# A two-layer diffusion trunk on one core: row sums for four scale tiles in the opening, and a fixed order of splits and norm operations at four later places

## The chip, the cores and the metric

The kernel runs on one core of one Trainium2 chip. The metric is the device time of one execution in microseconds (us), lower is better. The core has a matrix engine (TensorE, PE; its weight loads are listed apart as PEld), a vector engine (VectorE, DVE), a scalar engine (ScalarE, ACT), GpSimd (POOL) and the queue of SyncE (SP), which issues most of the DMAs. Matrix products write PSUM, whose eight banks hold 128 x 512 words each.

## The reference

256 context tokens and 256 latent tokens of width 1024 pass through two layers. Layer 0 mixes tokens with a two-directional mLSTM, layer 1 with multi-head latent attention (MLA); each mixer is followed by a gated convolutional FFN, and around each sub-layer stands an adaptive LayerNorm, whose shift, scale and gate come from a condition vector:

```python
def _modulation(cond, w, b):
    m = jax.nn.silu(cond) @ w + b
    return jnp.split(m[:, None, :], 6, axis=-1)      # shift, scale, gate, shift, scale, gate

for i in range(DEPTH):                               # DEPTH = 2
    ml = _modulation(c, ada_w[i], ada_b[i])          # latent
    mc = _modulation(c_ctx[None, :], ada_w[i], ada_b[i])   # context
    hl = x * (1 + ml[1]) + ml[0]
    hc = xc * (1 + mc[1]) + mc[0]
    yl, yc = mlstm(hl, hc) if i == 0 else mla(hl, hc)
    x = layer_norm(ALPHA * x + ml[2] * yl)
    f = conv_ffn(x * (1 + ml[4]) + ml[3])
    x = layer_norm(ALPHA * x + ml[5] * f)
    ...                                              # xc the same in layer 0
```

The mLSTM starts with `h @ w_up` (1024 to 2048 columns) and ends with `... @ w_out`; the MLA ends with its own `w_out`. In the kernel these products are called up, mout and aout, the FFN's fin0, fout0, fin1 and fout1.

## The kernel before

Everything is float32. Each operand x of a product is split in two parts, hi, rounded to the format of the matrix engine, and lo = x - hi, and a product is three matrix products (`mm3`: hi hi, hi lo, lo hi). For weights, hi is a cast on ACT (L340) and lo a subtraction on DVE (L343). `Stream` handles this for all weights in one fixed order: `_load` issues the DMA of the next 128 x 1024 tile into a free raw buffer, `_split` makes the two parts, `use` hands out a tile and splits up to `AHEAD` = 8 tiles in advance, and `pump(limit)` splits up to an index. Three buffers "w" hold split tiles; tiles marked wide go to "wu" in a larger pool.

The order of instructions on PE, DVE, ACT and SP is written out by hand in the opening (`manual_schedule`), on PE also from fout0 to the first part of `mla`. Elsewhere a planner orders each engine by the order of the program and its own estimate of times; `high_priority`, `issue_after` and `keep_in_program_order` bind it.

**The opening** (`start_up`) forms h of the first norm tile by tile and multiplies with six columns of w_up's blocks. For each of the eight 128-row tiles f:

- `load(f)`: two 512 KB tiles of the modulation weights (`adaw`, four k-blocks each of 128 shift and 128 scale columns), the transposed tokens `xT`, and the weights `raw0`.
- `ada_hi`, `ada_lo` or `ada_split`: both modulation tiles are split (ACT cast, DVE subtraction).
- `ada_rows` (L501): 16 products, the condition (4 columns: hi and lo of the two conditions) as stationary operand, 256 moving columns each; `ada_copy` (ACT) and `ada_T` (two transposes on PE) make columns of them, `ada_cols` adds the bias (DVE).
- `mod`: `mod_tile` applies shift and scale, half on DVE and half on ACT, then the split of h.
- `wsplit`: the split of the six weight blocks, ACT and DVE.
- `part(f, ms)`: three products of 512 columns for each block m, 18 for a tile, in six PSUM banks `ps`.

`warm(n)` issues n products of zeros. The other modulation columns are computed later in the background: `ada_bg` (L538) multiplies a transposed weight tile with the condition, broadcast to all rows (`bc`), and sums along the row on DVE; `tick` takes such steps from `bg2` at a rate n2 per product group (`ADA_U`, `ADA_Q`, `ADA_M`, `ADA_F`).

**mout** multiplies the normed heads with 16 weight tiles, for context (`pc`) and then latent tokens (`pl`); in its first half the last head (`head(3)`, `post`) is still being computed. `after0` is the norm behind it: `ln_rows`, then `ln_T`, which transposes (`zT`, L1255), scales (`zm`, L1262, L1264) and splits (`h`, L1267, L1268) the eight column blocks, two at a time; `tail` selects the variant in which the second block of a pair is scaled on DVE. `ctx_T` in `mla` is the same for the context tokens of layer 1.

**mla** forms keys, values and queries (`queries`, `qn`, L1756), then runs eight heads: `scores`, `trans` (transposes PT and their split), `attend` (o). It yields the list `oT` when head 6 is done and again after head 7; the caller issues aout in between, with `TAIL["aout"]` = 7 of the eight k-blocks held back for the end. Behind it, `st.limit = fi + QA` and `st.pump(fi + QC)` govern how many tiles of fin1 are split before and after the norm of aout.

Of the kernel before, what the change touches and what calls it, by code (L numbers as in the profile page):

```python
# [7 lines left out]
F32 = mybir.dt.float32  # L8
# [28 lines left out]
QA, QB, QC = 2, 4, 6  # L37
# [8 lines left out]
NUP = 6  # L46

# [86 lines left out]
def _pack(i):  # L134
# [73 lines left out]
    for k, v in parts.items():  # L208
# [21 lines left out]
                                     ).reshape(8, 2, 128, 1024),  # L230
# [8 lines left out]
class Stream:  # L239
# [73 lines left out]
    def _split(self):  # L313
# [19 lines left out]
        if key[0] == "gates":  # L333
# [42 lines left out]
class K:  # L376
# [98 lines left out]
    def ada_hi(self, f, h):  # L475
        hi, lo = [self.pool.tile([128, 1024], F32R, tag="u", name="adas", bufs=NU) for _ in range(2)]
        self.nc.scalar.copy(hi, self.adaw[f, h])
        self.adas[f, h] = hi, lo

    def ada_lo(self, f, h):  # L480
        hi, lo = self.adas[f, h]
        self.nc.vector.tensor_sub(lo, self.adaw.pop((f, h)), hi)
# [3 lines left out]

    def ada_split(self, f, h):
        hi, lo = [self.pool.tile([128, 1024], F32R, tag="u", name="adas", bufs=NU) for _ in range(2)]
        w = self.adaw.pop((f, h))
        for c in self.cuts(f):  # L490
            self.split(hi[:, c], lo[:, c], w[:, c])
        self.adas[f, h] = hi, lo

    def ada_rows(self, f):

        nc = self.nc
        self.adap[f] = pr = self.ps("adar")
        for k in range(8):
            c = slice((k % 4) * 256, (k % 4 + 1) * 256)
            for x in self.adas[f, k // 4]:  # L500
                nc.tensor.matmul(pr[0:4, 0:256], self.condr[:, k, :], x[:, c],  # L501
                                 start=k == 0 and x is self.adas[f, 0][0], stop=k == 7 and x is self.adas[f, 1][1])
        del self.adas[f, 0], self.adas[f, 1]

    def ada_copy(self, f):
        self.adar[f] = r = self.s2("adarow")
        self.nc.scalar.copy(r[0:4, 0:256], self.adap[f][0:4, 0:256])

    def ada_T(self, f):
        r = self.adar.pop(f)  # L510
        for i in range(2):
# [3 lines left out]
    def ada_cols(self, f):  # L515
        nc = self.nc
        t = self.tiny(4, "adt").rearrange("p (c b) -> p c b", c=2)
        p = self.adap.pop(f)[:, 256:264].rearrange("p (c b) -> p c b", c=2)
        b = self.smc("ada_b").rearrange("p (c f) -> p c f", c=2)[:, :, f:f + 1].to_broadcast([128, 2, 2])
        nc.vector.tensor_tensor(t, p[:, :, 2:4], b, op=ALU.add)  # L520
        nc.vector.tensor_tensor(self.mod0[:, :, f, :], p[:, :, 0:2], t, op=ALU.add)
# [41 lines left out]

    def ada_all(self, items):

        nc = self.nc
        self.bc = []
        for j in range(2):
            r = self.pool.tile([128, 1024], F32, tag="acc", name="bc", bufs=2)
            self.gate(r[0:1, 0:1])  # L570
            nc.sync.dma_start(r, self.a["crow"][j:j + 1, :].to_broadcast([128, 1024]))
            self.bc.append(r)
# [6 lines left out]
        for r in self.bc:  # L579
            nc.scalar.activation(r, r, AF.Silu)  # L580
# [23 lines left out]
    def start_up(self):  # L604
# [8 lines left out]
        self.adaw, self.adas, self.adap, self.adar, self.xT = {}, {}, {}, {}, []  # L613

        def load(f):
            for h in range(2):
                t = self.uf("adaw")
                for c in self.cuts(f):
                    nc.sync.dma_start(t[:, c], self.a["adaf"][f, h][:, c])
                self.adaw[f, h] = t  # L620
            x = self.s2("xT")
            nc.sync.dma_start(x, self.a["tokT"][f])
            self.xT.append(x)
            tag, bufs = ("ar", 2) if f in (3, 4) else ("raw", NRAW)
            r = self.pool.tile([128, 1024], F32, tag=tag, name="raw0", bufs=bufs)
            nc.sync.dma_start(r[:, :NUP * 128], st.ws[st.ids["upf", f, 0][0], :, :NUP * 128])
            raws.append(r)
# [1409 lines left out]
```

## Time and profile before

| what | value |
|---|---|
| median of 3 runs | 1383.55 us (1381.83 to 1386.48) |
| profiled execution, time / span | 1382.18 / 1380.4 us |
| instructions in the span | 19253 |
| busy: PE, DVE, ACT, POOL | 98%, 77%, 51%, 9% |
| DMA | 291.86 MB, mean 211 GB/s |

Times in the trace count from the start of the span. A row of a group names line, engine, operation, output and input tile, shapes and count, then busy time and the mean of one, then the idle time before it and what ended it. A matrix product's busy time runs to its modelled end, and products overlap; their spacing is what they cost. A row of the waits reads: engine and line that waited, what ended the wait, total us, number of waits, the longest. A row of windows gives, for a stretch, its length, busy time and number of instructions of PE, PEld, DVE, ACT and POOL, then granted clock of PE (1.00 is full), busy share of the DMA engines and GB/s.

### The profile page before, as it was taken

The page shows a single profiled execution, that of the slowest core. Times are in us where ns is not written, and L with a number is a line of the kernel's source. Part 1 is how long each engine was busy: PE and PEld are TensorE (multiplying, and loading weights), DVE is VectorE, ACT ScalarE, POOL GpSimd, SP SyncE. Part 2 cuts the span into 40 slices and gives each one's busy share as a digit, 9 for nine tenths or more (in the row PEclk, how much of TensorE's full clock was granted, in tenths as well). Part 3 has the DMA queues.
Part 4 walks back from the last instruction along what each step waited for, and adds up shares of the span by engine and source line. Part 5 has one row for each costly group of instructions (what it writes and reads, how often), then busy time and mean ns, then how long its engine had stood idle before and what let it go on. Part 6 is the DMA issues. An engine that isn't in the chain of part 4 may idle for free.

```text
span 1380.4 us, 19253 instructions
## 1 busy us (share of the span) xinstructions
PE 1355.3 (98%) x6966; PEld 1146.1 (83%) x6966; DVE 1063.3 (77%) x1722; ACT 705.5 (51%) x1197; POOL 122.5 (9%) x215
## 2 busy tenths in 40 slices
PE   8999999999999999999999999999999999999997
PEld 5788888888788888878798888888879888899986
DVE  6698856687688697779789878668887888877773
ACT  6695443445544545375643433334566665555560
POOL 0032000011011011110002000001100010000000
PEclk9999999999999999999999999999999999999999
DMA  9679848788666374656737867636866415467650
GB/s 362 221 275 326 298 171 254 233 285 291 221 208 202 110 230 148 225 193 214 258 130 267 283 220 248 224 115 194 257 217 204 152 69 176 138 190 231 205 185 31
DMA packets 88334, 291.86 MB, mean 211 GB/s; under 512 B 11656, under 2 KB 12296, under 8 KB 88240
## 3 DMA queue, kind: packets, MB, share of 16 engines
q1 hardware_dynamic: 62128, 215.64, 46.6%
q0 software_dynamic: 17472, 57.57, 13.5%
q10 hardware_dynamic: 8640, 17.44, 3.4%
q8 instruction: 54, 0.88, 0.3%
q14 instruction: 40, 0.33, 0.1%
HBM read 260.02 MB, written 30.58 MB: 211 GB/s over the span
## 4 chain that ended last, share of the span: by engine, by line
PE 90%; DVE 5%; ACT 2%; DMA 2%; issue 1%; DVEq 0%; SPq 0%; ACTq 0%
PE fin L404 9%; PE fin L405 9%; PE fin L406 9%; PE y L1444 7%; PE tok L404 6%; PE tok L406 6%; PE tok L405 6%; PE qk L404 4%; PE qk L406 4%; PE qk L405 4%; PE y L405 3%; PE y L406 3%; PE y L404 3%; PE up L404 2%; PE up L405 2%; PE up L406 2%
## 5 line engine op out<-in xcount | busy, mean ns | idle before, releaser
L343 DVE TENSOR_TENSOR w<-raw,w 128x1024 fp32r<-128x1024 f32 (+1 forms) x285 | 342.9, 1206 | 149.2 <-ACT w L340 146.4
L340 ACT CAST w<-raw 128x1024 fp32r<-128x1024 f32 (+1 forms) x285 | 295.7, 1039 | 295.6 <-PE fin L406 87.1
L405 PE MATMUL fin<-h,w 128*128 128x256 f32 (+1 forms) x696 | 231.8, 333 | 0.0
L406 PE MATMUL fin<-h,w 128*128 128x256 f32 (+1 forms) x696 | 231.5, 333 | 0.0
L404 PE MATMUL fin<-h,w 128*128 128x256 f32 (+1 forms) x696 | 231.4, 333 | 0.1
L538 DVE SCALAR_TENSOR_TENSOR junk<-ar,bc 128x1024 f32<-128x1024 f32 x128 | 155.7, 1216 | 7.9 <-ACT bc L580 5.5
L405 PEld LDWEIGHTS fin<-h,w 128*128 128x128 f32 x696 | 132.2, 190 | 12.9 <-DVE h L1268 0.2
L406 PEld LDWEIGHTS fin<-h,w 128*128 128x128 f32 x696 | 132.2, 190 | 12.9
L404 PEld LDWEIGHTS fin<-h,w 128*128 128x128 f32 x696 | 132.0, 190 | 13.1 <-ACT h L1267 0.3
L404 PE MATMUL qk<-xc,w 128*128 128x512 f32 x256 | 100.7, 393 | 0.0
L406 PE MATMUL qk<-xc,w 128*128 128x512 f32 x256 | 99.9, 390 | 0.0
L405 PE MATMUL qk<-xc,w 128*128 128x512 f32 x256 | 99.8, 390 | 0.0
L404 PEld LDWEIGHTS qk<-xc,w 128*128 128x128 f32 x256 | 48.1, 188 | 10.0 <-issue 0.4
L406 PEld LDWEIGHTS qk<-xc,w 128*128 128x128 f32 x256 | 48.1, 188 | 9.9
L405 PEld LDWEIGHTS qk<-xc,w 128*128 128x128 f32 x256 | 48.1, 188 | 9.7
L343 DVE TENSOR_TENSOR wu<-raw,wu 128x1024 fp32r<-128x1024 f32 (+3 forms) x37 | 42.7, 1177 | 12.7 <-ACT wu L340 12.4
L404 PE MATMUL up<-hT,w 128*128 128x512 f32 x128 | 50.8, 397 | 0.2 <-ACT hT L661 0.2
L405 PE MATMUL up<-hT,w 128*128 128x512 f32 x128 | 50.1, 391 | 0.2 <-DVE hT L664 0.2
L406 PE MATMUL up<-hT,w 128*128 128x512 f32 x128 | 49.9, 390 | 0.0
L404 PE MATMUL tok<-w,hT 128*128 128x512 f32 x128 | 49.8, 389 | 0.0
L405 PE MATMUL tok<-w,hT 128*128 128x512 f32 x128 | 49.8, 389 | 0.0
L406 PE MATMUL tok<-w,hT 128*128 128x512 f32 x128 | 49.8, 389 | 0.0
(438 smaller groups left out, 2982.0 us busy)
## 6 DMA issues: line engine op xcount, KB each, us to landing
raw<-in_ws SPq DMA_DIRECT2D x281, 512.0 KB, 4.4
ar<-in_adaT SPq DMA_DIRECT2D x80, 512.0 KB, 4.5
adaw<-in_adaf SPq DMA_DIRECT2D x14, 512.0 KB, 8.4
raw<-in_ws POOLq DMA_DIRECT2D x13, 512.0 KB, 7.6
raw<-in_ws SPq DMA_DIRECT2D x12, 384.0 KB, 8.4
xmd<-xr POOLq DMA_DIRECT2D x16, 256.0 KB, 5.3
xcd<-cv POOLq DMA_DIRECT2D x16, 256.0 KB, 5.6
xs<-xmd POOLq DMA_DIRECT2D x16, 256.0 KB, 6.4
```

The lines of the kernel that those rows point to most:

```text
L340: k.nc.scalar.copy(h[:, :cols], src)
L343: k.nc.vector.tensor_sub(l[:, :cols], src, h[:, :cols])
L404: mm(out, w[0], x[0], start=start, stop=False)
L405: mm(out, w[0], x[1], start=False, stop=False)
L406: mm(out, w[1], x[0], start=False, stop=stop)
L538: nc.vector.scalar_tensor_tensor(o, w, 1.0, self.bc[j], op0=ALU.mult, op1=ALU.mult, accum_out=col[:, k, j:j + 1])
L1444: nc.tensor.matmul(ps[b], a[:, p, ts], w[q][:, cs], start=j == 0 and n == 0 and not more, stop=j == 10 and n == 2, skip_group_check=True)
```

## The change

Opening. The condition rows `bc` are made at the start by 16 transposes on PE of a broadcast column and four copies out of PSUM (three on DVE, one on ACT), in place of two broadcast DMAs and two Silu operations later. Tiles 0 to 3 (`NFD` = 4) keep the scheme of before. For tiles 4 to 7 `ada_rows` has only the 128 shift columns (one modulation tile split, 16 products of 128 columns), and the scale column is two row sums on DVE (`ada_sum`), with a transposed weight tile. The low part of the weights of tiles 1 to 7 is subtracted on POOL. `warm` is gone, and the order of all operations is written anew, POOL's as well; the rest of the small constants is loaded after tile 2 in place of tile 0.

Later places. The splits of mout get a high priority, and mout's ticks take no more background steps. In `ln_T` with `tail`, the first block's subtraction comes after the second block's scaling, for layer 1 the order is pinned, and `la`, `lv` point to the sixth block's split. In `mla` the splits go only as far as the second query tile before `ctx_T` and the others are issued after its sixth block; the evacuation of the queries has a high priority; `trans` of the last head comes before `yield`, and aout's first block is issued before `attend` of head 6. `QA` goes from 2 to 3.

```diff
+FIRST = {'mout': 50}
+LNQ = 5
+QP = 40
-QA, QB, QC = 2, 4, 6
+QA, QB, QC = 3, 4, 6
+NFD = 4
 ...
-        if key[0] == "gates":
+        if key[0] in FIRST:
+            with k.tc.high_priority(FIRST[key[0]]):
+                k.nc.scalar.copy(h[:, :cols], src)
+                k.nc.vector.tensor_sub(l[:, :cols], src, h[:, :cols])
+        elif key[0] == "gates":
 ...
     def ada_rows(self, f):
+        nh = 2 if f < NFD else 1
+        n = 128 * nh
         for k in range(8):
-            c = slice((k % 4) * 256, (k % 4 + 1) * 256)
-            for x in self.adas[f, k // 4]:
-                nc.tensor.matmul(pr[0:4, 0:256], self.condr[:, k, :], x[:, c],
+            kk = k % (8 // nh)
+            for x in self.adas[f, k * nh // 8]:
+                nc.tensor.matmul(pr[0:4, 0:n], self.condr[:, k, :], x[:, kk * n:(kk + 1) * n],
 ...
+    def ada_sum(self, f, j):
+        w = self.adat[f]
+        o = self.pool.tile([128, 1024], F32, tag="junk", name="junk", bufs=1)
+        col = self.mod0[:, 1, f, :]
+        nc.vector.scalar_tensor_tensor(o, w, 1.0, self.bc[j], op0=ALU.mult, op1=ALU.mult, accum_out=col[:, j:j + 1])
+        if j:
+            del self.adat[f]
+            b = self.smc("ada_b")[:, 8 + f:9 + f].to_broadcast([128, 2])
+            nc.vector.tensor_tensor(col, col, b, op=ALU.add)
 ...
+        def w_lo(f):
+            t, n = w[f], NUP * 128
+            (nc.gpsimd if f > 0 else nc.vector).tensor_sub(t[:, 1, :n], raws[f][:, :n], t[:, 0, :n])
+            if f < 3:
+                load(f + 5)
 ...
+        def bc_rows(j):
+            for kt in range(8):
+                nc.tensor.transpose(ps[2 * j + kt // 4][:, kt % 4 * 128:(kt % 4 + 1) * 128],
+                                    self.cond[:, kt, j:j + 1].to_broadcast([128, 128]), self.ident)
 ...
             for f in range(1, 8):
+                part(f, range(3))
 ...
                 if f < 7:
-                    self.ada_copy(f + 1)
+                    w_hi(f + 1)
+                    w_lo(f + 1)
+                    mod(f + 1)
+                if 1 < f < 6:
+                    self.ada_lo(f + 2, 0)
+                if f < 7:
+                    h_lo(f + 1)
                 if f < 6:
-                    self.ada_split(f + 2, 0)
-                    self.ada_hi(f + 2, 1)
-                part(f, range(2))
+                    for j in range(2 if f + 2 >= NFD else 0):
+                        self.ada_sum(f + 2, j)
+                    self.ada_rows(f + 2)
+                    self.ada_copy(f + 2)
+                if f < 5:
+                    self.ada_hi(f + 3, 0)
+                part(f, range(3, NUP))
 ...
                 hi, lo = dst(k)
-                nc.scalar.copy(hi, tmp[:, c])
-                nc.vector.tensor_sub(lo, tmp[:, c], hi)
+                ha = pin(nc.scalar.copy(hi, tmp[:, c]))
+                if not (tail and i == 0):
+                    if tail:
+                        hi0, lo0 = dst(k - 1)
+                        pin(nc.vector.tensor_sub(lo0, tmp[:, 0:256], hi0))
+                    hv = pin(nc.vector.tensor_sub(lo, tmp[:, c], hi))
+                    if k == LNQ:
+                        self.la, self.lv = ha, hv
 ...
-        st.limit = [x[0] for x in st.order].index(("aout", 0, 0))
+        end = [x[0] for x in st.order].index(("aout", 0, 0))
+        st.limit = [x[0] for x in st.order].index(("uqn", 0, 1)) + 1
 ...
+            with self.tc.high_priority(QP):
+                nc.scalar.activation(u[:, 0], ps, AF.Copy, scale=scale)
+                nc.vector.scalar_tensor_tensor(u[:, 1], ps, scale, u[:, 0], op0=ALU.mult, op1=ALU.subtract)
 ...
         ctx_T()
+        with self.tc.issue_after(self.lv.ins), self.tc.issue_after(self.la.ins):
+            st.pump(end)
 ...
-            if 1 <= h < H1:
-                st.pump(ao + h)
+            if 1 <= h < H1 - 1:
+                st.pump(ao + h + h // 6)
 ...
+            if h == H1:
+                yield oT
             if h >= 2:
                 attend(h - 2, PTs.pop(h - 2))
+        PT = trans(H1 - 1, Ps.pop(H1 - 1))
         yield oT
-        attend(H1 - 1, trans(H1 - 1, Ps.pop(H1 - 1)))
+        attend(H1 - 1, PT)
 ...
-            k.outmm("mout", range(i, i + 1), hn, pc, 0, 16, 2, n2=ADA_M)
+            k.outmm("mout", range(i, i + 1), hn, pc, 0, 16, 2)
 ...
-            yield from k.ln_T(zs, A, B, dst, g == 1)
+            yield from k.ln_T(zs, A, B, dst, 0 if g == 0 else 1 + l)
 ...
-        k.outmm("aout", range(8 - TAIL["aout"]), o1, pl, 0, 8, 1)
+        k.outmm("aout", range(1), o1, pl, 0, 8, 1)
+        next(att)
+        k.outmm("aout", range(1, 8 - TAIL["aout"]), o1, pl, 0, 8, 1)
         next(att)
```

More of the change, by code (lines that the diff above doesn't have):

```diff
@@ L481, in ada_lo @@
         hi, lo = self.adas[f, h]
-        self.nc.vector.tensor_sub(lo, self.adaw.pop((f, h)), hi)
+        w = self.adaw.pop((f, h))
+        for c in self.cuts(f):
+            self.nc.vector.tensor_sub(lo[:, c], w[:, c], hi[:, c])
     def cuts(self, f):
         return (slice(0, 512), slice(512, 1024)) if f == 0 else (slice(0, 1024),)
[L487 to L492, printed above, removed]
     def ada_rows(self, f):
@@ L578, in ada_all @@
             yield
-        for r in self.bc:
-            nc.scalar.activation(r, r, AF.Silu)
+        if first:
+            self.bc_silu()
         yield
```

170 lines of the change are left out of this document (97 added, 73 removed).

## The prediction

> **What bounds the kernel now.** I read the page first, then the waits of the matrix engine (PE), then the timeline and windows of the five places that the change touches.
>
> ```profile
> span 1380.4 us, 19253 instructions
> PE 1355.3 (98%) x6966; PEld 1146.1 (83%) x6966; DVE 1063.3 (77%) x1722; ACT 705.5 (51%) x1197; POOL 122.5 (9%) x215
> PE 90%; DVE 5%; ACT 2%; DMA 2%; issue 1%; DVEq 0%; SPq 0%; ACTq 0%
> ```
>
> PE is busy for 98% of the span, and 90% of the chain that ended last is PE's. So time can come only from fewer or shorter PE instructions, or from the 25 us (1380.4 - 1355.3) in which PE stands still. Who it waits for:
>
> ```profile
> PE adar L501 <- ACT adas L409: 4.8, 1, 4.8
> PE zT L1255 <- DVE z L1227: 2.5, 1, 2.5
> PE y L405 <- DVE w L343: 1.3, 2, 1.1
> PE dkv L404 <- DVE qn L1756: 1.2, 1, 1.2
> PE o L404 <- ACT PT L409: 1.0, 1, 1.0
> PE y L405 <- DVE wu L343: 0.8, 1, 0.8
> PE fin L404 <- ACT h L1267: 0.6, 1, 0.6
> ```
>
> The first row is the first weights landing, which no edit shortens. The others belong to the norm of aout (z, fin), mout (y after w and wu), the context norm (dkv) and the last attention head (o): the places named in the change. Each is about 1 us, so this is a change of single microseconds.
>
> **The opening, from the fourth tile on.** Steady state of before:
>
> ```profile
> 27.81:34.20 6.39, 6.39 (x39) 4.77 (x37) 4.48 (x7) 4.22 (x6) 0.00 (x0) 1.00 1.03 403
> 28.15 0.40 PE L405 MATMUL up<-hT,w 128*128 128x512 f32 x1
> 28.39 0.39 PE L406 MATMUL up<-hT,w 128*128 128x512 f32 x1
> 32.24 1.92 PEld L501 LDWEIGHTS adar<-adas,condr 128*4 128x4 f32 x16
> 1154.79 0.87 PE PT L1800 x8
> ```
>
> The window is one tile's period; its columns are length, then busy time of PE, weight loads, DVE, ACT, POOL, granted clock, DMA share, GB/s. PE is busy for all 6.39 us: 18 products of 512 columns at a spacing of 0.23 (28.15 to 28.39) are 4.14, 16 row products of 256 columns are 1.92 (0.12 each), and the rest are two small transposes. For the last four tiles the row products get 128 columns. No row shows such a product with four weight columns. If it goes down with the columns it costs 0.06; the nearest row of that width, the eight 128-column transposes in 0.87, gives 0.109, but each of those also loads 128 weight columns. I take the middle, 0.085: 16 x (0.12 - 0.085) = 0.56 a tile, 2.2 us for four; bounds 0.7 and 3.8. The period becomes 6.39 - 0.56 = 5.8.
>
> DVE must keep up with that. Per tile it loses one split and the low part of w, and gains two row sums:
>
> ```profile
> L482 DVE TENSOR_TENSOR adas<-adaw,adas 128x1024 fp32r<-128x1024 f32 x1 | 1.2, 1218 | 0.0
> L637 DVE TENSOR_TENSOR w<-raw,w 128x768 fp32r<-128x768 f32 x1 | 1.0, 951 | 0.0
> L538 DVE SCALAR_TENSOR_TENSOR junk<-ar,bc 128x1024 f32<-128x1024 f32 x128 | 155.7, 1216 | 7.9 <-ACT bc L580 5.5
> L1219 POOL TENSOR_TENSOR z<-z,gr 128x512 f32<-128x512 f32 x1 | 1.4, 1422 | 82.9 <-ACT z L1218 82.9
> ```
>
> Before, it was 4.48 busy of 6.39 (the window). After: 4.48 - 1.22 - 0.95 + 2 x 1.22 + 0.2 for the bias = 4.95, under 5.8 but close. ACT loses a 1.05 us cast a tile. The low part of w goes to POOL: by L1219's 1.42 for 512 elements, 768 take 2.1 us, in a queue that is empty here (POOL 0.00 in the window), so nothing is queued behind; it waits for ACT's high part early in the period and is due at the period's end. Its cover is the 3.6 us left. SP issues the same bytes (two 512 KB tiles per tile, one of other layout); raw buffers come free about 1 us later, which matters little, as SP's later loads stand far ahead. The two broadcast loads of the condition rows and their two Silu fall away; nobody waits for them in steady state, so nothing.
>
> **The start.**
>
> ```profile
> 5.54 3.51 PE L501 MATMUL adar<-adas,condr 128*4 128x256 f32 x15 [0.35 <-DVE adas L410]
> 11.91 0.50 PE L404 MATMUL up<-hT,w 128*128 128x512 f32 x1 [0.23 <-ACT hT L661]
> 20.73 0.97 PE L501 MATMUL adar<-adas,condr 128*4 128x256 f32 x7 [0.28 <-DVE adas L482]
> 1179.68 2.01 PE L1255 MATMUL zT<-ident,z 128*128 128x128 f32 x12 [2.51 <-DVE z L1227]
> ```
>
> The first row products stand 0.23 apart, twice the 0.12 of later: PE is still at half speed here. Sixteen transposes of the condition are put ahead of them: at the slow 2.01 / 12 = 0.17 each 2.7 us, of which 1.4 lie in the wait for the first split (the 4.8 us of the first row of waits), so the row products end some 0.8 us later. Against this, part 0 and the row products of two tiles need 18 x 0.23 + 32 x 0.12 = 8.0 us from 11.9, but the last of them end only about 21.5 (20.73 and seven at 0.12); half of those 1.6 us of waits may go with DVE's w low parts. I set 0.8 lost and 0.8 gained, so nothing. The eight idle products (L651) go; if they held the clock up, the products from 11.9 run at half speed for a few us: 0 to 2.4 us. The copies of the rows out of PSUM (three on DVE, one on ACT) stand in gaps where DVE waits for ACT. Opening: 2.2 us gained, between 4.6 (3.8, and the transposes free) and -2.5 (0.7 less 0.8 less 2.4).
>
> **mout.**
>
> ```profile
> 604.00:670.00 66.00, 65.31 (x310) 53.23 (x309) 60.85 (x97) 37.82 (x66) 3.94 (x8) 1.00 0.70 228
> L538 DVE SCALAR_TENSOR_TENSOR junk<-ar,bc 128x1024 f32<-128x1024 f32 x13 | 15.7, 1211 | 0.0
> 882.00:938.00 56.00, 56.00 (x249) 46.38 (x248) 33.40 (x45) 19.90 (x25) 3.46 (x5) 1.00 0.44 136
> 938.00:960.00 22.00, 22.00 (x99) 18.22 (x98) 19.58 (x21) 9.36 (x10) 3.06 (x4) 1.00 0.69 211
> ```
>
> DVE is 92% busy here (60.85 of 66), and 15.7 us of it from 604 to 700 are 13 row sums, which the removed ticks (22 x 0.6) issued. They move into the end of fin0, where DVE is 60% busy (33.40 of 56), so they are covered; but the ticks of w_qk and fin0 make only 51 + 52 of 107 steps, so four steps (4.9 us) spill over to 938, where DVE is 89% busy. Three weight buffers hold 3 x 12 x 0.23 = 8 us of PE work there; I take 0.3 lost, between 0 and 4.9. Without these sums, and with mout's splits put first on ACT and DVE, the waits on w and wu (1.3 + 0.8) should go; next is late the last head's chain on DVE, which now stands behind the splits. I take 2.1, between 3 (if still smaller waits, of which PE has many under 0.6, go too) and -1 outside the rival below.
>
> **Context norm and last head.**
>
> ```profile
> 1079.59 0.80 DVE w L343
> 1080.72 1.22 DVE wu L343
> 1081.94 0.60 DVE qn L1756
> ```
>
> These are rows of the chain: two splits stand on DVE ahead of qn, and the 1.2 us wait of dkv follows. The change puts qn first and issues those splits only after the sixth column block of the norm. I take the 1.2; the same splits are then late by up to as much for uv and the queries (bounds 2.2, with the smaller waits around it, and -1). The last head: `trans` is issued ahead of `yield`, and 12 aout products stand ready beside `attend`; that fills the 1.0 us wait of o. I take 0.9 (1.0 and -0.5).
>
> **Norm of aout.**
>
> ```profile
> 1179.98 1.03 ACT L340 CAST w<-raw 128x1024 fp32r<-128x1024 f32 x1
> 1180.92 1.01 ACT L1262 ACTIVATE zm<-zT,lnB,lnA 128x256 f32<-128x256 f32 x2
> 1181.05 1.23 DVE L343 TENSOR_TENSOR w<-raw,w 128x1024 fp32r<-128x1024 f32 x1 [1.42 <-ACT w L340]
> 1180.60:1187.40 6.80, 6.17 (x28) 5.47 (x27) 6.35 (x14) 6.80 (x16) 0.00 (x0) 0.50 0.29 80
> ```
>
> The 2.5 us wait ahead of zT stays: none of its steps is touched. Behind it a cast of a later weight sits on ACT ahead of zm, and its subtraction on DVE ahead of the second zm. With the order pinned and that split released only by the sixth block, zm starts some 0.7 us earlier, and the 0.6 wait of fin shrinks: 1.4 in all, counting that clock 0.50 makes the first products slow. If the shorter gap kept the clock up, up to 3.1 more (half of the 6.17 us that PE is busy in that window).
>
> **Sum:** 2.2 + 2.1 + 1.2 + 0.9 + 1.4 - 0.3 = 7.5 us. The profiled execution took 1382.18 (span 1380.4 and 1.8 around it) and gives 1374.7; it lies 1.4 under the median 1383.55, so on the median 1376.0.
>
> **Rivals.** First: POOL and DVE keep each other out. The only two POOL products of the trace:
>
> ```profile
> 1369.84 0.68 DVE L1197 SCALAR_TENSOR_TENSOR z<-xres,z 128x512 f32<-128x512 f32 x1
> 1370.26 1.42 POOL L1219 TENSOR_TENSOR z<-z,gr 128x512 f32<-128x512 f32 x1 [82.94 <-ACT z L1218]
> 1371.61 0.42 DVE L1197 SCALAR_TENSOR_TENSOR z<-xres,z 128x256 f32<-128x256 f32 x1
> 1371.76 1.42 POOL L1220 TENSOR_TENSOR z<-z,br 128x512 f32<-128x512 f32 x1
> ```
>
> Each starts 0.26 us before a DVE operation with two SBUF inputs ends, and both take 1.42, so no row shows one undisturbed. If they exclude each other, DVE's 4.95 and POOL's 2.1 add to 7.05, a little less where DVE reads PSUM: a period of 6.9 against 6.39, four times, is 2.0 lost in place of 2.2 gained: 1380.2. It decides from the point where both together pass 5.8. The Trainium skill, "SBUF — State Buffer", section "SBUF: two separate sides", states such a lock, held for the whole instruction, between a GpSimd operation and a DVE operation with two SBUF inputs; by it this rival would hold, and the four rows do not contradict it. Against it: w's low part is due late and may use gaps.
>
> Second: a 128-column product streams at a quarter of the rate, as long as one of 512 columns, 0.23. Then 4 x 16 x (0.23 - 0.085) = 9.3 more: 1385.3. Nothing shows it: 256 columns cost 0.12, half of 512's 0.23.
>
> Third, and slower: mout's splits, put first, stand at the head of ACT and DVE while their loads are under way, and head 3's chain waits behind them.
>
> ```profile
> L343 DVE TENSOR_TENSOR w<-raw,w 128x1024 fp32r<-128x1024 f32 x25 | 30.3, 1216 | 5.0 <-ACT w L340 5.0
> L343 DVE TENSOR_TENSOR wu<-raw,wu 128x1024 fp32r<-128x1024 f32 x5 | 6.1, 1224 | 6.2 <-ACT wu L340 6.1
> ```
>
> From 604 to 700 DVE already stands 6.2 us before wu's splits and 5.0 before w's, waiting for the casts, which wait for their loads. If all 11.2 came to lie on the path and mout's 2.1 were not gained: 1376.0 + 2.1 + 11.2 = 1389.3; slower than before from 5.5 us blocked on. Against it: today those waits cost PE only 2.1.
>
> **Numbers.** Forecast 0.61, POOL against DVE 0.17, slow products 0.10, blocked queues 0.12. 0.3% is 4.2 us, about what a measurement of this kernel can tell from no change. Under 1379.4 lie 0.60 of the first and 0.08 of the second: 0.68. Within: 0.01, 0.09, 0.07, 0.02: 0.19. Above 1387.7: 0.03 and 0.10: 0.13. Range: the upper bounds of all terms (4.6 + 3 + 2.2 + 1.0 + 4.5 = 15.3) give 1368.3, and the runs spread by some us, so 1368; upward it takes in the slow products and the lower half of the blocked queues: 1387.
>
> **What would show it.** Period of the row products of tiles 4 to 7 near 5.8 (6.9 with POOL's low part of w among DVE's gaps: first rival; products 0.23 apart: second). No L538 between 600 and 690, four after fin0. Waits on w and wu in mout gone, none on hn or PT in their place (third rival). qn ahead of the splits, zm directly behind zT. The prediction is wrong if the time up to the first og product falls by less than 1 us, or if fout0's first products wait.

## The result, and the profile after

The changed kernel took 1378.04 us (median of 9 runs, 1374.73 to 1380.41) against 1384.28 us of before beside it: ratio 0.9955, 95% interval 0.9942 to 0.9968. In a second series of six runs it took 1375.80 against 1383.48: 0.9941 (0.9925 to 0.9956). It is 6 to 8 us faster. The forecast was 1376.0. That it came so close is in part luck, since the sum behind it came right by cancellation: the opening, which was to bring 2.2 us, loses, and the four later places bring more than was set down for them.

The first profile of the changed kernel is of its longest run, 1380.41 us. Its page:

```profile
span 1378.5 us, 19276 instructions
PE 1353.2 (98%) x6970; PEld 1149.0 (83%) x6970; DVE 1073.7 (78%) x1734; ACT 700.3 (51%) x1190; POOL 138.1 (10%) x222
```

PE's busy time fell by only 2.1 us (1355.3 to 1353.2), and its idle time, span less busy, rose from 25.1 to 25.3. (The second profile, `again` below, is of a faster run: 1349.2 busy of 1373.0.) PE's waits in the first:

```profile
PE up L700 <- DVE ident L459: 3.5, 1, 3.5
PE adar L508 <- DVE adas L494: 3.2, 2, 2.5
PE zT L1318 <- DVE z L1290: 2.3, 1, 2.3
PE y L1514 <- DVE w L352: 1.8, 3, 1.1
PE up L413 <- ACT hT L695: 1.8, 1, 1.8
PE y L1514 <- ACT w L349: 1.5, 1, 1.5
```

The rows that stood for mout (y after w and wu), the context norm (dkv), the last head (o) and the norm (fin) are gone, but for 0.3 us on wu: all four places did what the change was for. New are a wait of the row products for a split on DVE (adar, 2.5 in one piece), one of the first product for hT, and longer waits in fout0 (y L1514).

The table gives the length of each stage, worked out from the starts of the matrix products in one profiled execution of each kernel. "Start" is the first up product, "opening" from there to the 144th, "mout" from its first product to the first of fin0, "fout0" from the last fin0 product to the first dkv, "context" from the first to the last kn, "head" from the last s to the last o, "norm" from aout's last product to fin1's last. The lower kernels are the experiments.

| kernel | start | opening | mout | fout0 | context | head | norm | median, ratio to before (95%) |
|---|---|---|---|---|---|---|---|---|
| before | 11.91 | 49.95 | 106.72 | 105.17 | 39.16 | 11.67 | 134.99 | |
| changed | 12.48 | 52.23 | 103.34 | 108.67 | 37.07 | 10.17 | 132.76 | 1378.04, 0.9955 (0.9942-0.9968) |
| again | 11.63 | 51.27 | 102.83 | 106.09 | 37.08 | 10.18 | 132.72 | 1375.80, 0.9941 (0.9925-0.9956) |
| late_only | 11.73 | 49.97 | 103.23 | 105.13 | 37.07 | 10.17 | 132.70 | 1374.46, 0.9931 (0.9916-0.9946) |
| lo_dve | 12.72 | 50.68 | 103.60 | 107.03 | 37.08 | 10.17 | 132.69 | 1374.73, 0.9933 (0.9919-0.9946) |
| warm | 12.70 | 51.32 | 102.83 | 105.21 | 37.07 | 10.17 | 132.80 | 1374.94, 0.9932 (0.9919-0.9945) |
| ticks | 12.52 | 53.61 | 107.59 | 105.38 | 37.08 | 10.17 | 132.88 | 1381.24, 0.9981 (0.9969-0.9992) |
| nofirst | 14.84 | 49.59 | 104.91 | 107.29 | 37.07 | 10.17 | 132.69 | 1376.52, 0.9952 (0.9937-0.9967) |
| no_ctx | 12.14 | 49.96 | 103.64 | 105.85 | 38.91 | 10.17 | 131.68 | 1374.95, 0.9938 (0.9923-0.9953) |
| no_head | 14.13 | 49.16 | 103.45 | 105.91 | 37.09 | 11.69 | 131.68 | 1375.76, 0.9945 (0.9931-0.9959) |
| no_norm | 13.18 | 49.57 | 103.26 | 107.91 | 37.09 | 10.16 | 132.93 | 1376.26, 0.9942 (0.9929-0.9955) |
| mix | 15.04 | 52.34 | 103.34 | 105.15 | 37.07 | 10.17 | 132.79 | 1378.06, 0.9952 (0.9936-0.9968) |
| late_warm | 14.64 | 49.54 | 103.69 | 105.12 | 37.07 | 10.18 | 131.67 | 1374.38, 0.9927 (0.9912-0.9941) |
| best | 12.87 | 48.62 | 103.38 | 108.75 | 37.10 | 10.17 | 131.69 | 1374.82, 0.9937 (0.9923-0.9950) |

Two columns move on their own. The start lies anywhere between 11.6 and 15.0 us, also among kernels with one and the same opening (late_only, nofirst, no_head, late_warm). And fout0 takes 105.1 to 108.8 us, although kernels with the same code there differ as much as any (late_only 105.13, no_norm 107.91, best 108.75). A median of one kernel is therefore not good to 1 us, and a stage in the table is a better witness than a median wherever the two say different things. A late start also hides part of the opening (the same code took 49.97 after a start at 11.73 and 49.16 after one at 14.13).

**The opening.** The row products of 128 columns are as short as the lowest bound of the prediction had them:

```profile
31.88 1.12 PE L508 MATMUL adar<-adas,condr 128*4 128x128 f32 x16
```

Sixteen of them start within 0.9 us, 0.059 apart, against 0.12 for 256 columns. So PE has the time. It is DVE that doesn't. The low part of w on POOL with the cast on ACT that comes before it (first fence), and DVE's operations beside it (second):

```profile
30.02 0.82 ACT L675 CAST w<-raw 128x768 fp32r<-128x768 f32 x1
30.92 2.61 POOL L680 TENSOR_TENSOR w<-raw,w 128x768 fp32r<-128x768 f32 x1 [2.88 <-DMA raw<-in_ws]
35.07 1.84 POOL L680 TENSOR_TENSOR w<-raw,w 128x768 fp32r<-128x768 f32 x1 [1.54 <-ACT w L675]
```

```profile
30.28 0.41 DVE L627 TENSOR_SCALAR xT<-xT,mod 128x256 f32<-128x256 f32 x1
30.61 1.22 DVE L494 TENSOR_TENSOR adas<-adaw,adas 128x1024 fp32r<-128x1024 f32 x1
32.03 2.04 DVE L707 TENSOR_TENSOR hT<-xT,hT 128x512 fp32r<-128x512 f32 x1 [0.20 <-ACT hT L695]
34.00 1.21 DVE L539 SCALAR_TENSOR_TENSOR junk<-adat,bc 128x1024 f32<-128x1024 f32 x1
35.25 2.74 DVE L539 SCALAR_TENSOR_TENSOR junk<-adat,bc 128x1024 f32<-128x1024 f32 x1
```

At its shortest POOL's operation takes 1.84. At 30.92 it starts inside L494 and takes 2.61, 0.8 us longer, about the rest of L494. Then L707, 0.69 elsewhere, takes 2.04 and ends 0.5 us after POOL (34.07 and 33.53); the second L539 takes 2.74 in place of 1.21 and ends 1.1 us after POOL (37.99 and 36.91). Each waits for the other to the end of its operation. Two POOL operations fall close together here, since the first had to wait for ACT's cast of the same weights: it ended at 30.84, and as it began at 30.02, the raw weights, which the row of POOL names, had landed by then. Together they hold DVE up by 2.9 us (1.35 + 1.53), and PE, which needs tile 5's split behind them, stands 2.5 us:

```profile
40.10 1.76 PE L508 MATMUL adar<-adas,condr 128*4 128x128 f32 x15 [2.51 <-DVE adas L494]
```

That gap has a second price. The windows of the changed kernel show the granted clock (the number before the last two):

```profile
12.51:15.92 3.41, 3.41 (x7) 2.40 (x8) 3.41 (x4) 3.41 (x4) 0.79 (x1) 0.50 1.03 412
36.41:39.82 3.41, 1.18 (x6) 0.66 (x5) 3.30 (x7) 1.22 (x2) 0.50 (x1) 1.00 1.03 404
39.82:43.23 3.41, 3.13 (x19) 2.84 (x20) 3.34 (x7) 1.34 (x3) 0.00 (x0) 0.50 0.64 256
1176.46:1179.87 3.41, 1.10 (x10) 0.70 (x8) 2.30 (x7) 1.38 (x3) 0.00 (x0) 1.00 0.00 0
1179.87:1183.28 3.41, 3.41 (x16) 3.41 (x17) 1.71 (x4) 2.56 (x6) 0.00 (x0) 0.50 0.02 5
```

Behind a stretch of 3.41 us in which PE was busy for only 1.1 to 1.5, the next 3.41 us run at clock 0.5. Ahead of the last products before had one such stretch, of 6.8 us at the norm; the changed kernel has four of 3.41, two of them in the opening, one in fout0, one at the norm.

**mout.**

```profile
604.00:670.00 66.00, 66.00 (x316) 54.47 (x315) 56.75 (x95) 38.54 (x66) 6.00 (x12) 1.00 0.69 227
```

```profile
L560 DVE SCALAR_TENSOR_TENSOR junk<-ar,bc 128x1024 f32<-128x1024 f32 x7 | 8.5, 1213 | 0.0
```

DVE is down from 60.85 to 56.75 of 66 us, and 7 row sums are left of 13 between 604 and 700.

### The profile page after: what moved, and what is told of

It is laid out like the page before. It is cut to its first block, busy times and chain, and to the rows that moved or that the text cites. A ratio compares the mean times of both kernels' runs of the same rounds, so it can differ in the third digit from the quotient of the medians.

```text
span 1378.5 us, 19276 instructions
## 1 busy us (share of the span) xinstructions
PE 1353.2 (98%) x6970; PEld 1149.0 (83%) x6970; DVE 1073.7 (78%) x1734; ACT 700.3 (51%) x1190; POOL 138.1 (10%) x222
## 4 chain that ended last, share of the span: by engine, by line
PE 85%; DMA 5%; DVE 4%; ACT 2%; issue 2%; POOL 0%; SPq 0%; DVEq 0%; ACTq 0%; POOLq 0%
PE fin L413 9%; PE fin L414 9%; PE fin L415 9%; PE y L1514 6%; PE tok L414 5%; PE tok L415 5%; PE tok L413 5%; PE qk L413 4%; PE qk L415 4%; PE qk L414 4%; PE y L414 4%; PE y L413 4%; PE y L415 4%; DMA zr<-fd 2%; DMA raw<-in_ws 1%
## 5 line engine op out<-in xcount | busy, mean ns | idle before, releaser
L352 DVE TENSOR_TENSOR w<-raw,w 128x1024 fp32r<-128x1024 f32 (+1 forms) x258 | 310.1, 1205 | 129.2 <-ACT w L349 127.5
L349 ACT CAST w<-raw 128x1024 fp32r<-128x1024 f32 (+1 forms) x258 | 267.3, 1037 | 262.7 <-PE tok L415 85.3
L560 DVE SCALAR_TENSOR_TENSOR junk<-ar,bc 128x1024 f32<-128x1024 f32 x128 | 155.7, 1217 | 6.7 <-ACT bc L597 4.6
L1514 PE MATMUL y<-w,fz 128*128 128x512 f32 x198 | 48.7, 402 | 3.3 <-DVE w L352 1.8
L415 PE MATMUL tok<-w,hT 128*128 128x512 f32 x128 | 49.8, 389 | 0.0
L413 PE MATMUL tok<-w,hT 128*128 128x512 f32 x128 | 49.8, 389 | 0.0
```

The lines of the kernel that those rows point to most:

```text
L349: k.nc.scalar.copy(h[:, :cols], src)
L352: k.nc.vector.tensor_sub(l[:, :cols], src, h[:, :cols])
L413: mm(out, w[0], x[0], start=start, stop=False)
L415: mm(out, w[1], x[0], start=False, stop=stop)
L560: nc.vector.scalar_tensor_tensor(o, w, 1.0, self.bc[j], op0=ALU.mult, op1=ALU.mult, accum_out=col[:, k, j:j + 1])
L1514: nc.tensor.matmul(ps[b], a[:, p, ts], w[q][:, cs], start=j == 0 and n == 0 and not more, stop=j == 10 and n == 2, skip_group_check=True)
```

## The experiments

**late_only: the opening of before, everything else changed.**

```diff
 start_up, ada_rows, ada_all and the layout of their weights: as before
 FIRST, QP, QA = 3, ln_T, mla, aout: as changed
```

> The changed kernel with the opening of before (8 column tiles in 256-column row products, idle products, no POOL) and all later parts of the change. My sum gave the new opening 2.2 us of gain: by it this kernel is 2.2 us slower than the changed kernel, 1380.2. By what the two traces show (first up product +0.54, the 144th up product +2.8 us later in the changed kernel) the new opening costs 2.8 us: this kernel is 2.8 us faster than the changed kernel, 1375.2, and its 144th up product starts near 61.9. A third way: the lateness of the opening is taken back behind it (og waits for its tok tiles anyway, 0.7 us of it came back there), then within 1 us of the changed kernel.

1374.46 us, the 144th up product at 61.71. The second reading holds: the later parts alone are worth 9.5 us (1383.91 to 1374.46), and the new opening gives part of it back: 52.23 against 49.97 in one profile, 51.27 against 49.97 in the other (again, with nearly the same start), so 1.3 to 2.3 us, and 1.3 to 3.6 by the medians.

**lo_dve: POOL left out.**

```diff
-            (nc.gpsimd if f > 0 else nc.vector).tensor_sub(t[:, 1, :n], raws[f][:, :n], t[:, 0, :n])
+            nc.vector.tensor_sub(t[:, 1, :n], raws[f][:, :n], t[:, 0, :n])
```

> The changed kernel with the low part of w of all tiles on DVE, none on POOL. Theory (POOL and DVE shut each other out): the POOL operation of 1.84 us stretches DVE operations by about its own length, so that taking it away frees more of DVE (1.84 a tile) than the 0.95 us operation put back costs: the period of the row products falls from about 6.8 to about 6.0, the 144th up product starts 2 to 4 us earlier, 1374 to 1376. Rival (no lock; the stretched DVE operations had another cause, for instance PSUM or DMA writes): DVE gets 0.95 us a tile more, 7 tiles, and the time is equal or up to 4 us longer, 1378 to 1382, with the long DVE operations still there.

Three periods of the last tiles (transposes L521 at 37.34 and 55.19) take 17.85 us. A window of that length, which begins 3.1 us earlier:

```profile
34.21:52.08 17.87, 16.96 (x105) 12.87 (x106) 17.45 (x34) 9.50 (x15) 0.00 (x0) 1.00 0.62 217
```

DVE is busy for 17.45 of it, and for 17.43 from 37.34 to 55.19. The period is 5.95, nearly all DVE's work, and no DVE operation in it is longer than 1.23. The changed kernel needs 21.46 for the same three (35.04 and 56.50), before 19.16 (35.79 and 54.95). So POOL and DVE do shut each other out, and work on POOL made the opening longer. The 144th product came only 1.3 us earlier, short of the 2 to 4 expected, and the opening is 1.55 us shorter than in the first profile (0.6 than in the second, which has one stretch at half clock less): the period is right, but the tile before those three took 7.29 (30.05 to 37.34), because DVE stood 1.25 us there for ACT's cast of w, a wait that in the changed kernel is POOL's. The median of 1374.73 lies in the theory's range. Of the two theories the lock holds; its size at the end of the opening was overrated.

**warm: the idle products back.**

```diff
             self.ada_copy(0)
             bc_out(nc.scalar.copy, 1)
+            warm(2)
             self.ada_T(0)
+            warm(6)
```

> The changed kernel with the eight idle products of before put back around the transposes of the first row products. The trace of the changed kernel shows the granted clock at 0.5 from 12.5 to 15.9 us, just behind the place where they were. Theory: they hold the clock up, no such window, and the 144th up product starts 1 to 1.7 us earlier: 1376.5. Rival: DVE sets the end of the opening, the slow products are hidden behind it: no difference (within 0.5 us), whether or not the window goes.

The stretch at half clock near 12.5 is gone and the opening is 0.9 us shorter (51.32): the theory, and the median of 1374.94 is below its 1376.5. The second profile of the changed kernel (again, below) has neither the idle products nor that stretch, and an opening of 51.27. There PE stands still for 2.5 us in all around the first up product, but a border of the clock's windows, at 10.72, cuts that into 1.3 and 1.1; with the idle products no window there has more than 0.6. Of the four profiles with this opening and without the products (changed, again, lo_dve, ticks) three have the stretch. The other runs have no trace, but their mean clock is on record: 0.996 to 0.997 in all six runs of warm, 0.994 to 0.995 in 11 of the 15 runs of the changed kernel, on average 0.0012 lower, which is what one stretch of 3.41 us at 0.5 takes off the mean (the mean doesn't say where in the run). So the products hold the clock up here; without them it depends on where the gap falls, and in most runs the stretch seems to come. The other stretch, behind the 2.5 us wait of tile 5, stays.

With lo_dve this accounts for the opening: 52.23 less 1.55 for POOL and 0.9 for the idle products is 49.8, an estimate, since no run has both edits. Before has 49.95.

**ticks: mout's row sums back, its splits still first.**

```diff
-            k.outmm("mout", range(i, i + 1), hn, pc, 0, 16, 2)
+            k.outmm("mout", range(i, i + 1), hn, pc, 0, 16, 2, n2=ADA_M)
 ...
-        k.outmm("mout", range(8, 12), hn, pc, 0, 16, 1)
+        k.outmm("mout", range(8, 12), hn, pc, 0, 16, 1, n2=ADA_M)
```

> The changed kernel with the row sums issued in mout's first two calls again (12 ticks of 0.6 steps, 7.2 row sums of 1.21 us on DVE). If mout's gain (0.65 us in its second half, and 2.7 us in the context half) comes from the row sums that went, 2 to 3.4 us of it go again: 1380 to 1381.4, and waits on w, wu or hn come back in mout. If it comes from the splits put first (priority 50), nothing changes: within 0.5 us of the changed kernel.

1381.24 us, mout 107.59 against 103.34: the first theory, and more than its 3.4. It is even longer than before (106.72). The wait, in the waits of PE:

```profile
PE hnT L1231 <- DVE oh L1225: 2.6, 1, 2.6
```

oh is the output of head 2, which `post` still has to scale on DVE while head 3 is computed. With the row sums back, the splits put first push it back until PE stands 2.6 us, and a stretch at half clock follows.

**nofirst: late_only without the priority of mout's splits.**

```diff
-FIRST = {'mout': 50}
+FIRST = {}
```

> The changed kernel with the opening of before (as late_only) and mout's splits no longer put first. Restoring the row sums cost 4.3 us in the context half of mout with the splits first, where before, with the row sums and without that priority, it was 2.7 us longer than the changed kernel. So the priority looks worth -1.5 us beside the row sums. Theory A (the row sums are the whole gain, and the priority only pushes head 3's chain back): 0 to 1 us faster than late_only, 1373.5 to 1374.5, mout's two halves no longer than in late_only. Theory B (the priority is what takes the waits on w and wu away): those waits come back, 1 to 2 us longer in mout, 1375.5 to 1376.5.

mout 104.91 against 103.23, and a wait is back:

```profile
PE y L412 <- DVE w L350: 1.1, 1, 1.1
```

Theory B. With late_only and ticks beside it the two halves of the edit come apart: taking the row sums out alone is worth 1.8 us (106.72 to 104.91), the priority alone costs 0.9 (106.72 to 107.59), both together are worth 3.5 (106.72 to 103.23).

**no_ctx, no_head, no_norm: late_only with one later place undone each.**

```diff
 no_ctx:  st.limit = index of ("aout", 0, 0); no high_priority around qn; no issue_after
 no_head: attend(H1 - 1, trans(H1 - 1, ...)) behind the yield; all ready aout blocks in one call;
          st.pump(ao + h) for each head, as before
 no_norm: QA = 2; ln_T without pin; each low part directly behind its high part
```

> late_only with the context norm's part of the change undone (splits of w and wu issued at once again, no priority for qn). My sum gave 1.2 us; the step from the first to the last kn product shrank by 2.1 us in the changed kernel. Theory: the step grows by 2.1 again, dkv waits for qn, 1376.5. Rival: the 2.1 us belong to the splits' place in the norm's own order, which stays here: half of it or less comes back, 1374.5 to 1375.5.

> late_only with the part of the last attention head undone (the transposes of the last head behind the yield again, all ready aout products in one go, the splits paced as before). My sum gave 0.9 us; the step from the last s to the last o product shrank by 1.5. Theory: it grows by 1.5 again with a wait of o for PT near 1 us, 1376.0. If half or more of that was only moved (o earlier, aout's products no earlier), less than 0.8 us in the median.

> late_only with the order of the norm of aout undone (one fewer later split ahead of fin1 held back, zm and the casts not pinned, the two low parts in their old order). The changed kernel's gain here lay in the clock: one stretch of 3.41 us at 0.5 behind the norm instead of two. Theory (the gap before zT and fin sets how many such stretches follow): the wait of fin for h (0.6 us) comes back and with it the second stretch: 2 to 2.5 us longer to the end of fin1, 1376.5 to 1377. Rival (the length of the half clock depends on when the norm starts, not on this order): only the 0.6 us come back, 1375.0.

The waits that came back, first no_ctx, then no_head:

```profile
PE dkv L411 <- DVE qn L1770: 1.2, 1, 1.2
```

```profile
PE o L411 <- ACT PT L416: 1.0, 1, 1.0
```

no_ctx: the stage grew by 1.84, as the theory had it. The median rose by only 0.5, since the norm of aout was 1.0 us shorter (131.68 against 132.70), for a reason that has nothing to do with the context norm and is shown under late_warm. no_head: 1.52, median 1375.76; nothing was only moved. no_norm: 0.23 (132.93 against 132.70), and neither the wait of fin nor a second stretch at half clock came back: the rival is right about the clock, and even its 0.6 is too much. The median of 1376.26 would fit the theory, but in the profiled run the time lies in the start and in fout0. The order of the norm is worth 0.2 us by itself. The other 2.1 us of that place (134.99 to 132.93) came with other parts of the change; which of them took the cast off ACT that stood ahead of zm isn't separated: it comes back in none of nofirst, no_ctx, no_head and no_norm.

**late_warm: fourteen transposes that nothing needs, in the gap ahead of zT.**

```diff
             pt = self.ps("zT")
+            for _ in range(NID if kp == 0 and tail > 1 else 0):
+                nc.tensor.transpose(pt[:, 0:128], self.ident, self.ident)
```

> late_only with fourteen transposes of the identity on PE ahead of the first transpose of the norm of aout (1.5 us of work that nothing needs, in the 2.3 us in which PE waits for z). Theory (a window of 3.41 us in which PE stands still for over 1.7 us is followed by one at clock 0.5): no half clock behind the norm, the stretch from the first to the last fin1 product 126.9 us as in the kernels where the gap fell across two windows (127.6 in late_only), the end 0.6 to 1.2 us earlier, 1373.3 to 1374. Rival (the half clock follows the start of the norm, whatever PE does in the gap): the stretch at 0.5 stays and nothing is gained, 1374.5; if the transposes push zT back, 0.5 slower.

Theory. PE's wait for z shrinks to 0.9, and the clock stays up behind it (windows of late_warm):

```profile
1172.40:1175.80 3.40, 2.48 (x24) 2.24 (x22) 2.30 (x7) 1.21 (x3) 0.00 (x0) 1.00 0.02 5
1174.20:1177.60 3.40, 2.37 (x18) 1.89 (x17) 1.75 (x6) 2.52 (x6) 0.00 (x0) 1.00 0.00 0
```

From the first to the last fin1 product it takes 126.86 (127.61 in late_only), and from aout's last product 131.67 against 132.70: 1.0 us gained by work that nothing needs. It isn't the place of the gap that does it here: borders of this run's windows lie at 1172.84 and 1176.25 (whole windows back from its only change of clock, at 1367.40), so the 2.3 us up to 1175.30 would have lain within one. The median, 1374.38, shows no gain beside late_only's 1374.46 and misses the 1373.3 to 1374 expected. no_ctx reaches the same 131.68 with the full 2.3 us wait; there the gap falls across the border of two windows:

```profile
1174.04:1177.45 3.41, 1.62 (x13) 1.39 (x13) 1.74 (x7) 2.08 (x4) 0.00 (x0) 1.00 0.02 5
1177.45:1180.86 3.41, 3.41 (x27) 3.35 (x28) 2.93 (x7) 2.97 (x8) 0.00 (x0) 1.00 0.00 0
```

**again: the changed kernel once more.**

> The changed kernel once more, beside the two above. In its first profile fout0 had 3.5 us of waits on its weights and on z that no other kernel with the same fout0 had in full (1.6 to 3.5 less), and three more stretches at half clock. Theory (the first profile was an unlucky execution, the opening costs 3.1 us): median 1377 to 1378, 3 us over late_only's 1374.5, the opening's milestones as in the first profile (144th up product 64.7), fout0 1.5 to 3.5 us shorter. Rival (fout0's waits belong to this kernel: its loads come 3 us late after the longer opening): fout0 as long as in the first profile, median 1379 to 1380.

1375.80 us; fout0 2.6 us shorter, with these waits of PE there, where the first profile had 1.8 and 1.5:

```profile
PE y L1514 <- ACT w L349: 1.5, 1, 1.5
PE y L1514 <- DVE w L352: 0.7, 2, 0.5
```

The first theory holds for fout0: most of its 3.5 us belonged to that execution (best, with another opening, has 108.75 again). The median lies below both ranges, and the opening's 64.7 didn't repeat (62.90), since the start was 0.9 earlier and one stretch at half clock less followed it.

**mix: row sums in the opening of before, nothing on POOL.**

```diff
 tiles 0 to 3 and the order of each tile: as before, idle products too
+            self.bc_load(False)                      # two broadcast loads behind tile 4's
 in the loop, behind the low part of w:
+                    for j in range(2 if f + 2 >= NFD else 0):
+                        self.ada_sum(f + 2, j)
```

> All later parts of the change, the order of the opening of before (with its idle products, nothing on POOL), and the row sums for the scale columns of the last four tiles; the condition rows come by two broadcast loads behind tile 4's and a Silu, not by transposes. DVE's work for such a tile adds to 5.94 us (the period measured with the low part of w on DVE), against 6.39 of PE's before. Theory (row sums are worth 0.45 us a tile once POOL and the start are out of the way): 144th up product 1.8 us earlier than late_only, near 59.8, and the median 1 to 2 us under late_only, 1372.5 to 1373.5. Rival (the extra megabyte of broadcast rows delays tile 5, since DMA is busy to 1.0 until 43 us): the 144th up product no earlier than 61.6, waits of ACT for adaw in the period, 1374.5 to 1376.

1378.06 us, opening 52.34: both theories fell. The megabyte did no harm, but the period was 7.02 (transposes L521 at 37.82 and 44.84), not 5.94. DVE in mix:

```profile
48.47 0.41 DVE L627 TENSOR_SCALAR xT<-xT,mod 128x256 f32<-128x256 f32 x1
49.75 0.69 DVE L707 TENSOR_TENSOR hT<-xT,hT 128x512 fp32r<-128x512 f32 x1 [0.87 <-ACT hT L695]
```

In each period DVE stands 0.9 us for ACT's cast of hT. In before's schedule there was slack for that; with two row sums more there isn't.

**best: mix with that gap filled, and the transposes of late_warm.**

```diff
-                    hi_lo(f + 2, 0)
+                    self.ada_hi(f + 2, 0)
                     if f + 2 < NFD:
+                        self.ada_lo(f + 2, 0)
                         self.ada_hi(f + 2, 1)
 ...
                     mod(f + 1)
-                    if f + 2 < NFD:
-                        self.ada_lo(f + 2, 1)
+                    if f < 6:
+                        self.ada_lo(f + 2, 1 if f + 2 < NFD else 0)
                     h_lo(f + 1)
```

> mix with one step moved and with the fourteen transposes of late_warm. In mix the period of the last tiles came out at 7.03 us, not 5.94, because DVE stands 1.1 us between the modulation and the low part of hT, waiting for ACT's two operations on hT. Here the low part of the scale tile (1.22 us on DVE) stands in that gap. Theory: DVE has no gap left, period 5.94, the stretch from the first to the 144th up product 1.5 to 2 us under the 49.97 of late_only (near 48.2), 126.9 in fin1, median 1372 to 1373. Rival (the row sums of the last tiles then come too late for the next modulation, and PE waits for hT again): period over 6.39, stretch no shorter than 50, median 1374 to 1376.

Opening 48.62, the shortest of all, 1.35 under late_only; up to 0.4 of that can be its later start (no_norm, which starts another 0.3 later, has 49.57). One of its periods:

```profile
39.62:45.09 5.47, 5.47 (x36) 4.35 (x35) 5.33 (x11) 2.72 (x6) 0.00 (x0) 1.00 1.03 406
```

PE is busy all the time again, in 5.47 where before had 6.39; the four periods up to 53.65 average 5.65. The median, 1374.82, is not under that of late_only or late_warm: fout0, 3.6 us longer than in late_only, and a start 1.1 us later took it back in the profiled run. The medians of late_only, late_warm and best lie 1.0 to 3.7 us under the changed kernel's two, but their intervals overlap that of its second series. Only late_warm ran beside that series (1372.87 to 1375.10 against 1374.86 to 1378.08), so for the other two a gain over the changed kernel is likely rather than shown. Among the three these runs can't choose.

## Why the prediction was right, and where it was wrong

**The sum.** Against before, the second profile of the changed kernel has: start 0.3 earlier, opening 1.3 longer, 0.2 longer from there to mout, mout 3.9 shorter, fout0 0.9 longer, context norm 2.1, head 1.5 and norm 2.3 shorter, 0.1 longer behind fin1. That is, but for rounding, the 7.4 by which the span fell (1380.4 to 1373.0). The forecast said 7.5. Its term for the opening was 3.5 too good; those for mout, context norm, head and norm were 1.8, 0.9, 0.6 and 0.9 too small, and 1.1 ahead of mout and in fout0 was in no term.

**Opening, +2.2 set, -1.3 to -2.3 measured. The step that failed is the cover of POOL's work, and beside it the clock at the start.** The 0.085 for a product of 128 columns was too high (0.059), an error in favour of the change. DVE's own sum was right: 4.95, with the 0.95 of w back on DVE 5.90, and lo_dve ran at 5.95. But I let the low part of w go to POOL for nothing, due "at the period's end" with 3.6 us to spare. That was the first rival, at 0.17, and its mechanism is what happened, with a period of 6.75 on average over the last four tiles against its 6.9, though unevenly: 5.5, 9.6 (35.04 to 44.61), 5.6 and 6.3, because POOL's operations sometimes fell into DVE's gaps and sometimes on two long ones in a row. POOL cost 1.55 us (lo_dve). The Trainium skill, "SBUF — State Buffer", section "SBUF: two separate sides", states the lock; here the trace agrees, with 0.69 turned into 2.04 and 1.21 into 2.74. I had four rows that didn't contradict it and should have given it more than 0.17. The "nothing" at the start was about right in `again` (0.3 earlier up to the first product). But the half clock there, allowed as 0 to 2.4 and set at nothing in the sum, came, by the clocks, in most runs and cost 0.9 (warm).

**Slow products.** Wrong, as the row at 31.88 shows.

**mout, 2.1 set, 3.4 to 3.9 measured.** The waits on w and wu went, as said, to 0.3 us. But I misread the diff: n2 is dropped in the first two calls only, 12 product groups, 7.2 steps and not 13 (the description of the change above says it too broadly as well). So 6 row sums went and 7 stayed between 604 and 700, against "none", nothing spilled past fin0 (the last L560 is at 914.5), and the 0.3 for it was spent on nothing. The term was too small because the parts help each other: neither alone gives more than 1.8 (nofirst, ticks).

**Blocked queues.** The third rival's mechanism is real, with a price of 0.9 us (ticks, including a stretch at half clock), but only while the row sums are there. Taking them away is what made the priority safe.

**Context norm, 1.2 set, 2.1 measured; last head, 0.9 set, 1.5 measured.** Right places and right waits; each was priced at the wait that the view names, and the smaller waits right behind it went too (in before six of the next spacings of dkv products were 0.20 to 0.38 us in place of 0.12, 0.9 together). What was mis-sized in both terms is the wait: the named one was taken for the whole.

**Norm of aout, 1.4 set, 2.2 measured, by another cause.** The order is worth 0.2: without the pinned order, and with QA back at 2, no_norm has no cast ahead of zm either, so neither is needed to move it. The rest is mostly one stretch at half clock instead of two, which stood in the prediction only as "up to 3.1 more".

**Named signs.** qn is ahead of the splits and zm directly behind zT. The time up to the first og product did not fall by 1 us but rose by 2.9 in the first profile and 1.0 in the second: the prediction named this as what would make it wrong, and for the opening it was.

## What to carry to other kernels

Before work goes to an idle GpSimd, add its time to DVE's in the same period, as if they were one engine; if the sum passes the period, leave it on DVE (here 4.95 + 1.84 = 6.8, against 5.9 with all of it on DVE). The wait that a view names can be less than its removal is worth (1.2 named and 2.1 gained in the context norm). A gap on PE can have a second price in the clock, which depends on where it falls and makes single profiles differ by a microsecond or two. Undo each part alone, and in pairs where two parts touch one queue: here one half of an edit cost 0.9 us alone and brought 1.7 with the other.

## What the runs showed of the hardware

The granted clock goes by windows of 3.41 us on a fixed grid: the stretches between two of its changes are whole multiples of that (in before 1170.77, 6.83 and 187.73 us, 343, 2 and 55 times 3.413). In the fourteen profiles, between 8.5 us and the last product, 23 windows at full clock had PE standing still for 1.7 to 2.6 us and were followed by one at 0.5. Two with 1.8 were not (no_ctx, no_head), and none with less than 1.6 was. A window at 0.5 is mostly followed by one at 1.0; in two cases, with 0.5 and 0.6 us of standing still in it (ticks, before), a second at 0.5 came. The Trainium skill, "TensorE: Matmul & The Clock Gate", section "HAM oscillation — how this bites in real kernels", gives as the rule no idle gaps over about 3.4 us. These runs disagree: about half of that is enough if it lies within one window, and the measurement decides.

Not only operations with two inputs wait for POOL: L627, one 256-column input from SBUF, took 1.55 us beside POOL in place of 0.41, while the two operations just ahead of it, which read PSUM, took their usual 0.15. The Trainium skill, "SBUF — State Buffer", section "SBUF: two separate sides", names, beside operations with two SBUF inputs, those in a two-port mode; no run here shows which mode L627 is in.

```profile
26.25 0.15 DVE L530 TENSOR_TENSOR adt<-adar,sm 128x4 f32<-128x4 f32 x1
26.44 0.16 DVE L531 TENSOR_TENSOR mod<-adar,adt 128x4 f32<-128x4 f32 x1
26.64 1.55 DVE L627 TENSOR_SCALAR xT<-xT,mod 128x256 f32<-128x256 f32 x1
```
